# Which engine makes the low halves of the weight splits: thirteen units from DMA to VectorE, one unit in which the heads pause, and two subtractions of w_out one unit later

## The chip, the cores and the metric

The kernel runs on one core of one Trainium2 chip. The metric is the device time in microseconds (us) of one execution; of the kernel before three executions are shown, with a median of 689.74 us (689.03 to 690.15). One more execution was profiled.

## What is computed

One layer of a hybrid encoder on x of 512 tokens by 1024 channels, all in float32:

```
h = rmsnorm(x, norm_w)
proj = h @ w_in + b_in                      # 1024 x 11272
mq, mk, mv, mi, mf, mo, mz, sq, sk, sv, sz, gates = split(proj)
# branch A: matrix memory, 4 heads of 256, causal conv and SiLU on mq, mk
y_m = rmsnorm(mlstm(conv(mq), conv(mk), mv, mi, log_sigmoid(mf))) * sigmoid(mo) * silu(mz)
# branch B: stick-breaking attention, 8 heads of 128
y_s = stick_breaking(rmsnorm(sq), rmsnorm(sk), sv) * silu(sz)
merged = sigmoid(g_m) * (y_m @ w_proj_m) + sigmoid(g_s) * (y_s @ w_proj_s)
out = x + merged @ w_out
```

## The kernel before

**Units.** All large products are cut into units: 128 output channels with the whole depth of 1024, or 512 output channels with 256 of the depth. A unit's weights (512 KB) are loaded into a tile `stg` (three buffers), split there into a high part `wh` and a low part `wl` (three buffers each, rounded to float32r), and multiplied in three passes, high by high, high by low and low by high (`mm3`, L94 to L97). A full unit is 24 matmuls of 128x512, in two halves of 12. The units stand in one list and are worked in its order; the loop at L1498 counts them as c. E is 36 (L29). The places that matter here, by c:

- 40 to 43 (E+4 to E+7) are q of the second set of attention heads, 44 to 47 its k, 48 to 51 its SiLU gate z, 52 to 55 a part of the merge gates;
- 100 to 107 are w_proj_s, 108 to 115 w_proj_m (n_proj is 116), and behind them come the products with w_out, which are formed with sums and differences of its blocks (t1 to t4, L1224 to L1241).

**The two ways to make a low part.** `Unit.split` (L122) has ScalarE write the high part with one ACTIVATE. Then either VectorE subtracts (L101: `wl = st - wh`), or, where `by_dma` is set, ScalarE writes minus the high part into `wl` with a second ACTIVATE (L128), and a DMA that GpSimd issues adds the tile `st` to it (L129, 512 KB, accumulating). That DMA still reads `stg`, so the buffer comes free only when it has landed. L1197 chooses the units of the second kind: before, all eight of w_proj_m and sixteen around the second set's q, k, z and gates, c = 40 to 55.

**What sets the order.** Each engine works its queue in the order of the code. In step c the loop calls what is due in that step (the table `later`), evacuates the banks of unit c-1, calls `ahead(c)`, which splits unit c+2 and issues loads up to unit c+4, issues the first half of unit c's matmuls, then lets every active head do one step (L1528), and issues the second half. From c = 108 on `ahead` also runs ahead of the evacuation (L1506). A head is a generator (L471): its steps are query and key parts; scores; a scan chain over two row blocks on VectorE (L519, L520, L537); the chain over the two others; a store of the weights `ay` to DRAM; their reload as `az`; a step without work; the split of `az` into `ath` and `atl`; the product with v in two steps (`aps<-ath,vh` and so on), the last with L593 on VectorE. The set `REST` (L34) names the steps c in which heads do nothing.

**The k group's end.** Units 44 to 47 fill all four dense PSUM banks (`dps`). In step 48 VectorE reads the four banks (L388, `kraw`), ScalarE squares each (L405, sixteen instructions with their accumulator reads in two steps), GpSimd makes the reciprocal roots (L283, L284), and one step later VectorE scales `kraw` by them (L420). Unit 48 needs the first of those banks. The two halves of `kraw` are thus scaled in steps 49 and 50, and in step 50 TensorE transposes `kraw` for the next head (L482).

Of the kernel before, what the change touches and what calls it, by code (L numbers as in the profile page):

```python
# [28 lines left out]
E = 4 + FILL + 14 * PAIRS  # L29
# [1 line left out]
M_START = [E + n for n in (37, 41, 54, 60)]  # L31
GATES_PREP, GATES_START, GATES_SCAN = E - 3, E - 1, E + 26
TURNED = {("q", 0, 0), ("q", 0, 1), ("q", 1, 0), ("q", 1, 1), ("k", 0, 1), ("k", 1, 1)}
REST = {E + n for n in (48,)}  # L34
AHEAD, LOADS = 2, 4


# [1 line left out]
def tile_hybrid_layer(  # L39
# [93 lines left out]
    units = []  # L133
# [844 lines left out]
    class Pair:  # L978
# [24 lines left out]
        def at(self, c, fn, *a):  # L1003
            later.setdefault(c, []).append(lambda: fn(*a))
# [189 lines left out]

    chan_group(w_proj_m, 0, D, lambda k: ymp[k], pm_evac)
    n_proj = len(units)
    for un in units[n_proj - 8:] + units[E + 4:E + 20]:  # L1197
        un.by_dma = True


# [170 lines left out]
    for g in range(2):  # L1371
        at(-11 + g, w_load, "B22", g, "P5")
        at(-12 + 2 * g, w_load, "B12", g, "A")
        at(-9 + g, w_load, "B11", g, "A")
        at(-8 + 2 * g, t3, g)
        at(-6 + 2 * g, t2, g)
        at(-5 + 2 * g, t1, g)
        at(1 + g, t4, g)
# [119 lines left out]
    for c in range(N):  # L1498
# [29 lines left out]
        for g in list(act):  # L1528
            if c in REST:
                continue  # L1530
            if next(g, "end") == "end":
                act.remove(g)
        for e in list(pend):
            if c >= e[0] and e[2]():
                pend.remove(e)
                g = e[3]()
# [36 lines left out]
```

## Time and profile before

| | us |
|---|---|
| median of three executions | 689.74 |
| the profiled execution | 688.95 |
| its span, first to last instruction | 687.1 |
| TensorE matmuls busy in the span | 674.7 |
| VectorE busy | 483.2 |
| ScalarE busy | 384.4 |
| GpSimd busy | 128.7 |

The granted TensorE clock was 0.997 over the span. A row of the timeline gives start, duration, engine, line, operation, tiles written and read, and in brackets the idle time ahead of it with what ended it. Matmuls follow each other every 0.227 us, and their durations overlap, so a wait is read from the distance between two starts. DVE is VectorE, ACT is ScalarE, POOL is GpSimd, PE is TensorE, SP issues most of the DMAs.

### The profile page before, as it was taken

How to read it: one execution, taken by the hardware profiler on the slowest of the kernel's cores; microseconds unless marked ns; L12 is line 12 of the kernel's file. 1: busy time of each engine (PE TensorE's matmuls, PEld its weight loads, DVE VectorE, ACT ScalarE, POOL GpSimd, SP SyncE). 2: the span in 40 equal slices, each digit the busy share in tenths (PEclk: the TensorE clock that was granted, in tenths of full speed). 3: DMA queues.
4: the chain of work that ended last, by engine and by line, in shares of the span. 5: the costliest groups of instructions: out<-in, count | busy, mean ns of one | idle time of the engine just before them, and what ended most of it. 6: DMA issues, size and time to landing. Idle time of an engine off the chain costs nothing.

```text
span 687.1 us, 9385 instructions
## 1 busy us (share of the span) xinstructions
PE 674.7 (98%) x3114; PEld 560.6 (82%) x3114; DVE 483.2 (70%) x839; ACT 384.4 (56%) x715; POOL 128.7 (19%) x278
## 2 busy tenths in 40 slices
PE   8999999999998899999999999999999999999998
PEld 6888888878887788888888888888888888778876
DVE  6777778668568468878788655479964466355997
ACT  7576545477694675653654747344465854335451
POOL 4023121423382234310011011100000120111020
PEclk9999999999999999999999999999999999999999
DMA  7576793958999999738369532535344478998433
GB/s 251 141 235 161 245 248 90 231 176 188 264 247 249 254 241 254 211 115 207 93 123 199 128 107 62 156 94 145 83 137 148 128 221 260 238 260 209 145 81 103
DMA packets 136336, 122.47 MB, mean 178 GB/s; under 512 B 17578, under 2 KB 106052, under 8 KB 136288
## 3 DMA queue, kind: packets, MB, share of 16 engines
q1 hardware_dynamic: 129232, 101.82, 50.7%
q0 software_dynamic: 6912, 19.93, 15.6%
q8 instruction: 24, 0.39, 0.2%
q14 instruction: 24, 0.20, 0.1%
q10 hardware_dynamic: 144, 0.13, 0.1%
HBM read 83.00 MB, written 18.93 MB: 148 GB/s over the span
## 4 chain that ended last, share of the span: by engine, by line
PE 80%; DMA 9%; issue 3%; DVE 2%; ACT 2%; POOL 1%; SPq 1%; POOLq 0%; ACTq 0%; DVEq 0%
PE dps L97 19%; PE dps L95 19%; PE dps L96 19%; PE dps L971 5%; DMA wl<-stg 4%; PE aps L971 4%; PE aps L96 3%; PE aps L97 3%; PE aps L95 3%; DMA stg<-in_w_proj_m_dram 2%; DMA stg<-in_w_in_dram 2%; ACT sqj L405 1%; PE dps L1446 1%; PE dps L1447 1%; PE dps L1448 1%
## 5 line engine op out<-in xcount | busy, mean ns | idle before, releaser
L95 PE MATMUL dps<-hh,wh 128*128 128x512 f32 x448 | 176.1, 393 | 1.7 <-DVE kraw L388 1.7
L97 PE MATMUL dps<-hh,wl 128*128 128x512 f32 x448 | 175.2, 391 | 2.1 <-DMA wl<-stg 2.1
L96 PE MATMUL dps<-hl,wh 128*128 128x512 f32 x448 | 175.1, 391 | 0.0
L101 DVE TENSOR_TENSOR wl<-stg,wh 128x1024 fp32r<-128x1024 f32 x60 | 73.3, 1222 | 58.0 <-ACT wh L100 57.3
L97 PEld LDWEIGHTS dps<-hh,wl 128*128 128x128 f32 x448 | 84.5, 189 | 20.6 <-DMA wl<-stg 2.6
L95 PEld LDWEIGHTS dps<-hh,wh 128*128 128x128 f32 x448 | 84.4, 188 | 18.7 <-DVE kraw L388 2.1
L96 PEld LDWEIGHTS dps<-hl,wh 128*128 128x128 f32 x448 | 84.5, 189 | 16.8
L100 ACT ACTIVATE wh<-stg 128x1024 fp32r<-128x1024 f32 x60 | 63.0, 1052 | 20.1 <-PE dps L96 12.9
L127 ACT ACTIVATE wh<-stg 128x1024 fp32r<-128x1024 f32 x24 | 25.3, 1054 | 33.7 <-DMA stg<-in_w_proj_m_dram 13.1
L129 POOL DMA_DIRECT2D wl<-stg x24 | 21.2, 882 | 106.8 <-ACT wl L128 74.2
L743 ACT ACTIVATE tmp<-acc 128x512 f32<-128x512 f32 x16 | 10.1, 633 | 52.9 <-DVE acc L740 52.9
L95 PE MATMUL dps<-wh,hh 128*128 128x512 f32 x96 | 37.5, 391 | 0.0
L96 PE MATMUL dps<-wl,hh 128*128 128x512 f32 x96 | 37.4, 390 | 0.0
L97 PE MATMUL dps<-wh,hl 128*128 128x512 f32 x96 | 37.4, 390 | 0.0
L740 DVE SCALAR_TENSOR_TENSOR acc<-tmp,vec,acc 128x511 f32<-128x511 f32 (+2 forms) x48 | 36.0, 750 | 1.7
L97 PE MATMUL dps<-yh,wl 128*128 128x512 f32 x64 | 25.3, 395 | 1.5 <-DMA wl<-stg 1.5
L519 DVE TENSOR_TENSOR_SCAN om<-om 128x512 f32<-128x512 f32 (+3 forms) x32 | 26.3, 822 | 0.0
L128 ACT ACTIVATE wl<-stg 128x1024 fp32r<-128x1024 f32 x24 | 25.1, 1045 | 0.0
L96 PE MATMUL dps<-yl,wh 128*128 128x512 f32 x64 | 24.9, 390 | 0.0
L95 PE MATMUL dps<-yh,wh 128*128 128x512 f32 x64 | 24.9, 389 | 0.0
L101 DVE TENSOR_TENSOR atl<-az,ath 128x384 fp32r<-128x384 f32 (+1 forms) x24 | 13.8, 601 | 14.9 <-ACT ath L100 10.6
L863 ACT ACTIVATE hns<-aps,hst 128x256 f32<-128x256 f32 x16 | 7.6, 475 | 27.8 <-DVE hst L862 20.8
(303 smaller groups left out, 1547.9 us busy)
## 6 DMA issues: line engine op xcount, KB each, us to landing
stg<-in_w_in_dram SPq DMA_DIRECT2D x71, 512.0 KB, 4.9
wl<-stg POOLq DMA_DIRECT2D x24, 512.0 KB, 7.2
a_d<-ay SPq DMA_DIRECT2D x8, 640.0 KB
az<-a_d SPq DMA_DIRECT2D x32, 160.0 KB, 5.4
stg<-in_w_proj_s_dram SPq DMA_DIRECT2D x8, 512.0 KB
B<-in_w_out_dram SPq DMA_DIRECT2D x8, 512.0 KB, 12.9
stg<-in_w_proj_m_dram SPq DMA_DIRECT2D x8, 512.0 KB, 3.9
dst<-u POOLq DMA_DIRECT2D x12, 256.0 KB, 4.7
```

The lines of the kernel that those rows point to most:

```text
L95: nc.tensor.matmul(ps, ah, bh, start=first, stop=False)
L96: nc.tensor.matmul(ps, ah, bl, start=False, stop=False)
L97: nc.tensor.matmul(ps, al, bh, start=False, stop=last)
L100: nc.scalar.activation(hi, src, AF.Copy)
L101: nc.vector.tensor_tensor(lo, src, hi.bitcast(F32), op=OP.subtract)
L127: nc.scalar.activation(self.wh, self.st, AF.Copy)
L128: nc.scalar.activation(self.wl, self.st, AF.Copy, scale=-1.0)
L129: nc.gpsimd.dma_start(out=self.wl, in_=self.st, accum_op=OP.add)
L519: nc.vector.tensor_tensor_scan(back, back, back, 1.0, op0=OP.mult, op1=OP.bypass)
L740: nc.vector.scalar_tensor_tensor(acc[:, j:], t[:, 0:T - j], cw(3 - j, ch), acc[:, j:], op0=OP.mult, op1=OP.add)
L743: nc.scalar.activation(t, acc, AF.Sigmoid)
L971: nc.tensor.matmul(pr.bank[key, tb], a, w[:, i, :], start=begin and n == 0, stop=end and n == 2, skip_group_check=again)
```

## The change

Three lines are edited:

```
-REST = {E + n for n in (48,)}
+REST = {E + n for n in (11, 48)}
...
-    for un in units[n_proj - 8:] + units[E + 4:E + 20]:
+    for un in units[n_proj - 3:] + [units[E + n] for n in (4, 5, 6, 7, 9, 10, 11, 12)]:
         un.by_dma = True
...
-        at(-8 + 2 * g, t3, g)
+        at(-7 + 2 * g, t3, g)
```

Of the 24 units whose low part came by DMA, eleven keep it: 40 to 43, 45 to 48, and 113 to 115. Thirteen go over to VectorE: 44, 49 to 55, and 108 to 112. Each of these loses one ACTIVATE (L128) and one DMA of GpSimd (L129) and gains one subtraction on VectorE (L101). In step 47 the three heads then active do nothing, so each of their later steps comes one unit later. The difference t3 of two blocks of w_out is taken in steps 109 and 111 and no longer in 108 and 110.

VectorE around steps 47 and 48, before. The rows begin with the end of step 46 (`ay` is a head's transposed weights); `atl` to the second `ay` are step 47's head work, then step 48 evacuates the k group:

```order
L537 STREAM_TRANSPOSE ay<-a_all 128x4x32
L101 TENSOR_TENSOR atl<-az,ath 128x384
L519 SCALAR_TENSOR_TENSOR om<-om 128x256
L520 TENSOR_TENSOR a_all<-a_all,om 128x256
L537 STREAM_TRANSPOSE ay<-a_all 128x4x32 x2
L519 SCALAR_TENSOR_TENSOR om<-om 128x384
L520 TENSOR_TENSOR a_all<-a_all,om 128x384
L537 STREAM_TRANSPOSE ay<-a_all 128x4x32 x3
L388 TENSOR_TENSOR kraw<-dps,brow 128x512 x4
L432 STREAM_TRANSPOSE ty<-qraw 128x8x32 x4
```

The same place in the changed kernel:

```order
L537 STREAM_TRANSPOSE ay<-a_all 128x4x32
L101 TENSOR_TENSOR wl<-stg,wh 128x1024
L388 TENSOR_TENSOR kraw<-dps,brow 128x512 x4
L432 STREAM_TRANSPOSE ty<-qraw 128x8x32 x4
L101 TENSOR_TENSOR wl<-stg,wh 128x1024
L101 TENSOR_TENSOR atl<-az,ath 128x384
L519 SCALAR_TENSOR_TENSOR om<-om 128x256
L520 TENSOR_TENSOR a_all<-a_all,om 128x256
L537 STREAM_TRANSPOSE ay<-a_all 128x4x32 x2
L519 SCALAR_TENSOR_TENSOR om<-om 128x384
L520 TENSOR_TENSOR a_all<-a_all,om 128x384
L537 STREAM_TRANSPOSE ay<-a_all 128x4x32 x3
```

The seven rows of head work have moved behind the evacuation of `kraw`, and two low parts (units 49 and 50) stand in the queue, one ahead of the evacuation and one behind it.

VectorE in steps 49 and 50, as the difference of the two orders, from the end of step 48 on:

```order
+L374 SCALAR_TENSOR_TENSOR ys<-dps,bvec,tmp 128x512
+L420 TENSOR_SCALAR kraw<-kraw,rk 128x128 x8
+L101 TENSOR_TENSOR wl<-stg,wh 128x1024
 L593 TENSOR_TENSOR ys<-aps,ys 128x512
-L374 SCALAR_TENSOR_TENSOR ys<-dps,bvec,tmp 128x512
-L420 TENSOR_SCALAR kraw<-kraw,rk 128x128 x8
-L101 TENSOR_TENSOR atl<-az,ath 128x512
-L101 TENSOR_TENSOR atl<-az,ath 128x384
 L374 SCALAR_TENSOR_TENSOR ys<-dps,bvec,tmp 128x512
 L452 TENSOR_SCALAR tz<-tz,qkw 128x1024
 L420 TENSOR_SCALAR kraw<-kraw,rk 128x128 x8
+L101 TENSOR_TENSOR wl<-stg,wh 128x1024
```

The low part of unit 51 now stands ahead of the second scaling of `kraw`, that of unit 52 behind it, and the next head's `atl` (two rows) has gone behind both.

## The prediction

> **What bounds the kernel now.** I read the page first, then who waited for whom on TensorE, then TensorE's timeline around each wait.
>
> ```profile
> PE 674.7 (98%) x3114; PEld 560.6 (82%) x3114; DVE 483.2 (70%) x839; ACT 384.4 (56%) x715; POOL 128.7 (19%) x278
> ...
> PE dps L97 <- DMA wl<-stg: 3.6, 3, 2.1
> PE dps L95 <- DVE kraw L388: 1.7, 1, 1.7
> ```
>
> TensorE is busy for 98% of the span, and the change leaves every matmul in place. So it can gain only waits, and two kinds stand at its places: for low parts by DMA, three times, and for VectorE's read of a `kraw` bank, once.
>
> ```profile
> 214.87 0.39 PE L96 MATMUL dps<-wl,hh 128*128 128x512 f32 x1
> 215.09 0.39 PE L97 MATMUL dps<-wh,hl 128*128 128x512 f32 x1
> 217.21 0.50 PE L95 MATMUL dps<-hh,wh 128*128 128x512 f32 x1 [1.72 <-DVE kraw L388]
> ...
> 229.19 0.39 PE L96 MATMUL dps<-hl,wh 128*128 128x512 f32 x1
> 231.73 0.50 PE L97 MATMUL dps<-hh,wl 128*128 128x512 f32 x1 [2.15 <-DMA wl<-stg]
> ...
> 232.81 0.63 PE L97 MATMUL dps<-hh,wl 128*128 128x512 f32 x1
> ...
> 235.37 0.50 PE L97 MATMUL dps<-hh,wl 128*128 128x512 f32 x1
> 235.71 0.39 PE L95 MATMUL aps<-ath,vh 128*128 128x512 f32 x1
> ...
> 236.94 0.60 PE L482 MATMUL aps<-ident,kraw 128*128 128x128 f32 x4
> ...
> 599.24 0.39 PE L96 MATMUL dps<-yl,wh 128*128 128x512 f32 x1
> 600.47 0.50 PE L97 MATMUL dps<-yh,wl 128*128 128x512 f32 x1 [0.84 <-DMA wl<-stg]
> ...
> 616.70 0.39 PE L96 MATMUL dps<-yl,wh 128*128 128x512 f32 x1
> 617.73 0.50 PE L97 MATMUL dps<-yh,wl 128*128 128x512 f32 x1 [0.65 <-DMA wl<-stg]
> ```
>
> Starts normally lie 0.23 apart, so the four waits cost their distance less 0.23: 1.89 at unit 48's first matmul, 2.31 in unit 50, 1.00 in unit 108 and 0.80 in unit 111. After the longest the matmuls run slow: from 231.73 to 235.37 there are nine steps of matmuls, 3.64 us where nine at 0.227 take 2.04. That is another 1.60. The stretches show why (columns: PE, PEld, DVE, ACT, POOL, then the granted clock, the DMA share, GB/s):
>
> ```profile
> 208.00:218.00 10.00, 8.28 (x37) 6.60 (x36) 9.45 (x23) 3.15 (x7) 0.87 (x1) 1.00 1.02 259
> 232.00:236.00 4.00, 4.00 (x12) 3.13 (x12) 3.17 (x11) 1.83 (x3) 0.86 (x1) 0.57 1.04 234
> 590.00:606.00 16.00, 15.16 (x67) 12.26 (x66) 5.32 (x8) 5.22 (x7) 2.64 (x3) 1.00 1.01 233
> ```
>
> The clock fell to 0.57 behind the 2.15 us gap and stayed at 1.00 around the 1.72 us gap, so here it falls somewhere between the two. [...] The waits and the clock sum to 1.89 + 2.31 + 1.60 + 1.00 + 0.80 = 7.60 us. The DMA engines are full at both places.
>
> **The change: low parts of units 49 to 55 and 44 by VectorE.** One low part costs VectorE 1.22 us and spares ScalarE 1.05 us, a GpSimd issue and a transfer:
>
> ```profile
> L101 DVE TENSOR_TENSOR wl<-stg,wh 128x1024 fp32r<-128x1024 f32 x60 | 73.3, 1222 | 58.0 <-ACT wh L100 57.3
> L127 ACT ACTIVATE wh<-stg 128x1024 fp32r<-128x1024 f32 x24 | 25.3, 1054 | 33.7 <-DMA stg<-in_w_proj_m_dram 13.1
> L128 ACT ACTIVATE wl<-stg 128x1024 fp32r<-128x1024 f32 x24 | 25.1, 1045 | 0.0
> ...
> 222.75 8.94 DMA wl<-stg
> ...
> 590.46 9.96 DMA wl<-stg
> ...
> 608.87 8.81 DMA wl<-stg
> ```
>
> The first group row's own idle time says what VectorE's subtraction waits for, ScalarE's high part. The split is issued two units ahead, at least 10.9 us, so 1.22 us in place of 8.94 removes the 2.31 wait in unit 50, and the slow clock behind it. Unit 44's subtraction falls ahead of the chain of step 42, beside matmuls that need nothing of it soon; I cost it at nothing.
>
> **The pause in step 47.** VectorE's queue of that place before (rows as above: start, duration):
>
> ```profile
> 212.15 0.52 DVE L101 TENSOR_TENSOR atl<-az,ath 128x384 fp32r<-128x384 f32 x1
> ...
> 215.88 0.70 DVE L537 STREAM_TRANSPOSE ay<-a_all 128x128 f32<-128x128 f32 x3
> 216.50 2.44 DVE L388 TENSOR_TENSOR kraw<-dps,brow 128x512 f32<-128x512 f32 x4
> 218.87 1.40 DVE L432 STREAM_TRANSPOSE ty<-qraw 128x256 f32<-128x256 f32 x4
> 220.91 0.69 DVE L593 TENSOR_TENSOR ys<-aps,ys 128x512 f32<-128x512 f32 x1 [0.64 <-PE aps L97]
> ...
> 231.13 0.74 DVE L374 SCALAR_TENSOR_TENSOR ys<-dps,bvec,tmp 128x512 f32<-128x512 f32 x1
> 231.79 0.74 DVE L452 TENSOR_SCALAR tz<-tz,qkw 128x1024 f32<-128x1024 f32 x1
> 232.45 1.66 DVE L420 TENSOR_SCALAR kraw<-kraw,rk 128x128 f32<-128x128 f32 x8
> 234.02 0.55 DVE L101 TENSOR_TENSOR atl<-az,ath 128x384 fp32r<-128x384 f32 x1
> 234.49 0.69 DVE L101 TENSOR_TENSOR qtt<-tz,qtt 128x512 fp32r<-128x512 f32 x1
> ```
>
> Head work of 216.50 − 212.15 = 4.35 us stands ahead of `kraw`. Now only the low part of unit 49 does: 212.15 + 1.2 = 213.3, and the first bank is read by 213.95. On TensorE unit 47 loses six matmuls of its heads (235.71 to 236.94 are six such: 1.23), so its last one starts at 215.09 − 1.23 = 213.86 and unit 48 could start at 214.09. The 1.89 wait goes but for a tenth. The moved matmuls come back in unit 48, at no gain or loss.
>
> **What is late next.** ScalarE stands between `kraw` and the rest:
>
> ```profile
> 224.31 0.30 ACT L405 ACTIVATE sqj<-kraw 128x128 bf16<-128x128 f32 x1
> ...
> 227.42 0.19 ACT L405 ACTIVATION_READ_ACCUMULATOR sqj<-kraw 128x1 f32 x1
> ```
>
> The squares of two banks take 3.30 us (224.31 to 227.61). From 213.95 they end at 217.3, unit 50's high part at 218.3, its low part on VectorE at 219.5 (which stands idle for it from 217.0), the moved head work of 4.35 at 223.9. Then come L374 (0.7), the first scaling (1.6), unit 51's low part (1.2), L593 (0.6), L374 and L452 (0.66 each, their starts' distance) and the second scaling (1.6): 230.9. TensorE meanwhile: unit 48 takes 24 × 0.227 + 1.23 = 6.7 and ends at 220.8; unit 49 takes 5.45 and six smaller matmuls of 256 and 128 columns, about 1.23 × 384/896 = 0.53, and ends at 226.8; twelve matmuls later, at 229.5, it reaches the transposes of `kraw` (L482). They wait 230.9 − 229.5 = 1.4 us. The trace of before has this wait hidden: the second scaling ended at 234.02, and TensorE, without 2.31 + 1.60 of its own waits, would have come at 236.94 − 3.91 = 233.03. It can be nothing (if ScalarE's pieces close up by 1.4) or twice that, 2.8, if two more pieces of 0.7 slip in; I take 1.4.
>
> Steps 51 to 55 each get 1.22 us more on VectorE, and the last two steps of two heads come one unit later, where the next heads' scan chains stand. Step 52 then holds L374, L452, a low part, L593, two `atl` (1.1), a chain of 3.9 (the 4.35 above less its `atl`) and two splits (`qtt` and its like, 0.69 each): about 9.6 us in a unit of 7. The excess of 2.6 meets the 2.7 us by which the twelve matmuls of the next unit's first half run ahead of its scores. Bounds are 0 and 1.5 (one low part more than fits); I take 0.5, nearer to none because the excess just fits.
>
> [...] In the trace GpSimd's masks stretch beside VectorE's scan:
>
> ```profile
> 246.81 0.29 POOL L512 TENSOR_SCALAR_AFFINE_SELECT a_all<-a_all 128x128 f32<-128x128 f32 x1
> ...
> 251.45 1.43 POOL L509 TENSOR_SCALAR_AFFINE_SELECT om<-om 128x128 f32<-128x128 f32 x1
> ...
> 251.47 1.34 DVE L519 TENSOR_TENSOR_SCAN om<-om 128x512 f32<-128x512 f32 x1
> ```
>
> A mask of 0.29 can take 1.43, 1.14 more. If a new subtraction did that to a mask on the path of steps 51 to 55, it would be inside the 1.5. [...]
>
> **w_proj_m.** VectorE is busy 5.32 of 16 us there (row above), so 1.22 per unit has room, and low parts of units 108 and 111 are ready long ahead of use: 1.00 and 0.80 go. It also frees `stg` some 8 us earlier, where the load queue stood:
>
> ```profile
> SPq L120 <- DMA wl<-stg: 26.4, 5, 10.3
> ```
>
> SP waited 26.4 us in 585 to 625 for low parts to land. Units 113 to 115 keep the DMA; nine to ten us from issue fit into two units (10.9) less ScalarE's 2.1 only just, so between 0 and 0.8 may return; 0, since the full queue loses five transfers. t3 moves by a unit and is needed by t2 one step later; its 1.22 us lie in the same idle time.
>
> **Sum.** 7.60 − 0.1 − 1.4 − 0.5 = 5.6 us. Against the profiled execution, 688.95 us, that is 683.35. The median of before is 0.79 higher, so 684.1 us.
>
> **The rivals.**
> - No new wait: the chain through ScalarE and VectorE closes up. 689.74 − 7.6 = 682.1. For it speaks the load taken off ScalarE and the DMA engines; against it the 233.03 above. 0.18.
> - The wait at the transposes passes the length at which the clock falls. It takes another 1.0 us in the chain, say a reload or GpSimd's roots held up: 2.4 of wait and 1.6 of slow clock in place of 1.4, so 686.7. [...] 0.12.
> - The waits in w_proj_m are not for the low parts' route but for the full DMA engines, and the loads come late instead: 1.8 is not won, 685.9. Against it: SP's 26.4 us of waiting is for low parts. 0.06.
> - Slower: VectorE's queue stands. The subtraction waits for ScalarE, which waits for a load; if those of units 50 to 53 landed 3 us late each, the heads behind them would stand 12 us, less the 2.7 that TensorE has in hand, plus one fall of the clock: 10.9 lost against 7.6 won, 693.0. It decides from some 2.5 us a unit on. For it: the full DMA engines; against it: eight transfers fewer there. 0.05.
>
> **The numbers.** The forecast's own chance is 0.59. Its range: new waits from 0.3 to 3.5 us put it between 682.4 and 685.6. With the rivals but the slower one, and the executions of before lying 1.1 apart, the range is 681.5 to 687.0. A measurement of this kernel can tell about 0.2%, 1.4 us, from no change. Slower has 0.05 from the last rival, the same 0.05 from the tails of the others, faster 0.9.
>
> **What would show it.** Right: no TensorE wait for `wl<-stg`, none over 0.4 at unit 48, no stretch of low clock, and a new wait of about 1.4 at L482 near 230, named after VectorE's L420. Wrong: a low clock after that wait, TensorE waiting for `wl` from VectorE, or waits at scores (`ktt`) near 250 to 265 that sum to more than 1.5. A time over 688.4 would refute the sum as a whole.

## The result

The kernel after takes 681.7 us (median of 9 executions, 680.71 to 686.68) against 689.66 us of before (9 executions, 687.34 to 694.84): ratio 0.9898, 95% interval 0.9864 to 0.9932. The medians lie 8.0 us apart; the ratio stands for 7.0 us less (4.7 to 9.4). The forecast was 684.1, so the direction was right and the gain, by the medians, 2.4 us too small. Six more executions, made beside the last experiments below, gave 681.19 against 688.65: ratio 0.9902 (0.9869 to 0.9934).

The execution of after that was profiled took 686.68 us, one of two among the nine that lie some 5 us above the others. Its profile lost them near 145 us, ahead of everything that the change moves (where the other, 686.65, lost them is not on record); so one of the six later executions of the same kernel (680.82 us, span 679.1) stands beside it and is called the second profile.

From the page of after, first profile: the engines, the subtractions and the low-part DMAs.

```profile
PE 673.8 (98%) x3114; PEld 561.4 (82%) x3114; DVE 497.3 (73%) x852; ACT 372.5 (54%) x702; POOL 114.9 (17%) x265
L101 DVE TENSOR_TENSOR wl<-stg,wh 128x1024 fp32r<-128x1024 f32 x73 | 89.2, 1222 | 69.5 <-ACT wh L100 68.8
L129 POOL DMA_DIRECT2D wl<-stg x11 | 9.8, 888 | 89.6 <-DVE gback L1177 45.9
```

Thirteen subtractions of 1.22 us more (x60 to x73) and thirteen DMAs fewer (x24 to x11): the change did what it says. What TensorE still waits for behind the first 20 us, by the waits of PE in the second profile (total, times, longest, in us):

```profile
PE aps L482 <- DVE dst L420: 0.5, 1, 0.5
PE aps L96 <- DVE ktt L101: 0.4, 1, 0.4
PE aps L482 <- DVE kraw L420: 0.2, 1, 0.2
```

Neither `wl<-stg` nor `kraw L388` is left, and the one new wait, the last row, is 0.2. TensorE at the two places of the forecast, second profile:

```profile
213.92 0.39 PE L97 MATMUL dps<-wh,hl 128*128 128x512 f32 x1
214.14 0.39 PE L95 MATMUL dps<-hh,wh 128*128 128x512 f32 x1
...
229.49 0.40 PE L97 MATMUL dps<-hh,wl 128*128 128x512 f32 x1
229.72 0.49 PE L482 MATMUL aps<-ident,kraw 128*128 128x128 f32 x3
230.37 0.33 PE L482 MATMUL aps<-ident,kraw 128*128 128x128 f32 x1 [0.15 <-DVE kraw L420]
230.45 0.49 PE L95 MATMUL dps<-hh,wh 128*128 128x512 f32 x1
```

And VectorE there:

```profile
212.02 1.20 DVE L101 TENSOR_TENSOR wl<-stg,wh 128x1024 fp32r<-128x1024 f32 x1
213.13 2.48 DVE L388 TENSOR_TENSOR kraw<-dps,brow 128x512 f32<-128x512 f32 x4
...
227.92 0.75 DVE L374 SCALAR_TENSOR_TENSOR ys<-dps,bvec,tmp 128x512 f32<-128x512 f32 x1 [0.18 <-ACT tmp L372]
228.59 0.74 DVE L452 TENSOR_SCALAR tz<-tz,qkw 128x1024 f32<-128x1024 f32 x1
229.25 1.65 DVE L420 TENSOR_SCALAR kraw<-kraw,rk 128x128 f32<-128x128 f32 x8
```

Side by side, in us from the start of the span (each the first matmul of a unit by TensorE's timeline):

| | before | forecast | after, second profile |
|---|---|---|---|
| unit 47 | 208.64 | | 208.70 |
| unit 48 | 217.21 | 214.1 | 214.14 |
| unit 49 | 223.53 | 220.8 | 220.82 |
| unit 50 | 228.97 | 226.8 | 227.00 |
| second scaling of `kraw` ends | 234.11 | 230.9 | 230.90 |
| unit 57 | 281.77 | | 276.17 |
| unit 108 | 599.01 | | 593.40 |
| unit 115 | 639.45 | | 631.48 |

By unit 57 the gain is 5.60, nothing changes from there to 108, and in w_proj_m another 2.37 comes: 7.97 in all, of 8.0 between the spans (687.1 and 679.1).

**The 5 us near 145.** In the first profile TensorE waits for the scaled keys of the first set of heads, by its timeline:

```profile
145.12 0.39 PE L97 MATMUL dps<-hh,wl 128*128 128x512 f32 x1
147.94 0.47 PE L482 MATMUL aps<-ident,dst 128*128 128x128 f32 x1 [2.43 <-DVE dst L420]
```

The two stretches behind it, by the windows (start and end; then length, busy time of PE, of its weight loads PEld, of DVE, ACT and POOL; then the clock, third number from the end), run at half speed:

```profile
147.76:151.18 3.42, 2.93 (x9) 2.25 (x10) 3.42 (x11) 0.79 (x2) 0.00 (x0) 0.50 0.50 153
151.18:154.59 3.41, 3.41 (x10) 2.64 (x9) 0.41 (x1) 0.00 (x0) 0.00 (x0) 0.50 0.51 154
```

Ahead of it the chain of waits has the load of a unit's weights (start, duration), first in the first profile, then in the second:

```profile
131.41 9.08 DMA stg<-in_w_in_dram
```

```profile
130.07 7.41 DMA stg<-in_w_in_dram
```

It was issued 1.34 later and took 1.67 longer; ScalarE's squares stand in its queue behind the split of that unit, so the scaling came 3.0 later. Before has the same wait with 0.5 us in its profile. Why the load is later in some executions stays open.

### The profile page after: what moved, and what is told of

The parts are those of the page before. It is cut to its first block, busy times and chain, and to the rows that moved or that the text cites. A ratio compares the mean times of both kernels' runs of the same rounds, so it can differ in the third digit from the quotient of the medians.

```text
span 685.0 us, 9337 instructions
## 1 busy us (share of the span) xinstructions
PE 673.8 (98%) x3114; PEld 561.4 (82%) x3114; DVE 497.3 (73%) x852; ACT 372.5 (54%) x702; POOL 114.9 (17%) x265
## 4 chain that ended last, share of the span: by engine, by line
PE 91%; DMA 2%; DVE 2%; ACT 2%; issue 1%; POOL 1%; SPq 1%; DVEq 0%; ACTq 0%; POOLq 0%
PE dps L95 23%; PE dps L97 22%; PE dps L96 22%; PE dps L971 5%; PE aps L971 4%; PE aps L96 3%; PE aps L97 3%; PE aps L95 3%; DMA stg<-in_w_in_dram 2%; PE dps L1446 1%; PE dps L1448 1%; PE dps L1447 1%; ACT sqj L405 1%; PE aps L853 1%; PE aps L855 1%
## 5 line engine op out<-in xcount | busy, mean ns | idle before, releaser
L101 DVE TENSOR_TENSOR wl<-stg,wh 128x1024 fp32r<-128x1024 f32 x73 | 89.2, 1222 | 69.5 <-ACT wh L100 68.8
L100 ACT ACTIVATE wh<-stg 128x1024 fp32r<-128x1024 f32 x73 | 76.7, 1052 | 42.9 <-PE dps L96 22.5
L129 POOL DMA_DIRECT2D wl<-stg x11 | 9.8, 888 | 89.6 <-DVE gback L1177 45.9
L507 ACT ACTIVATE om<-aps,rq 128x512 f32<-128x512 f32 (+3 forms) x32 | 16.7, 523 | 14.3 <-PE aps L97 14.3
L509 POOL TENSOR_SCALAR_AFFINE_SELECT om<-om 128x128 f32<-128x128 f32 x32 | 14.5, 452 | 44.5 <-ACT om L507 44.3
L101 DVE TENSOR_TENSOR atl<-az,ath 128x384 fp32r<-128x384 f32 (+1 forms) x24 | 13.8, 603 | 10.4 <-ACT ath L100 6.1
```

The lines of the kernel that those rows point to most:

```text
L100: nc.scalar.activation(hi, src, AF.Copy)
L101: nc.vector.tensor_tensor(lo, src, hi.bitcast(F32), op=OP.subtract)
L129: nc.gpsimd.dma_start(out=self.wl, in_=self.st, accum_op=OP.add)
L507: nc.scalar.activation(om[:, 0:n], zp, AF.Sigmoid, scale=rn[:, h:h + 1])
L509: nc.gpsimd.affine_select(out=om[:, ts], in_=om[:, ts], compare_op=OP.is_gt, fill=1.0, base=0, channel_multiplier=1, pattern=[[-1, 128]])
```

## The experiments

"Ratio" is to the kernel before in the same group of executions, with its 95% interval. Three groups of four ran on three chips, with medians of before of 687.91 (29 executions), 688.73 (11) and 688.65 (11).

### The parts alone

**The pause alone.**

```
-REST = {E + n for n in (48,)}
+REST = {E + n for n in (11, 48)}
```

> The kernel before with the pause in step 47 alone; all 24 low parts stay with the DMA. Theory A (the transfer of unit 50's low part starts when ScalarE has squared the first kraw banks, so it starts as much earlier as kraw is read): the wait at unit 48's first matmul goes (-1.9 us), the one in unit 50 shrinks from 2.3 to about 1.6, and the clock no longer falls (-1.6): some 4 us faster, ratio near 0.994. Rival B (the full DMA engines set the landing, not the issue): TensorE only comes earlier to the same landing, waits some 4 us in unit 50, the clock falls as before, and the time stays within 1 us: ratio 0.999 to 1.001. In both the waits of 1.0 and 0.8 us in w_proj_m stay.

Measured: 689.01 us, ratio 1.0016 (0.9991 to 1.0042). Both theories fell. The waits at units 48 and 50 were gone in the profile, yet nothing was won, since a new wait stood at the scores of the next heads, and the clock fell behind it:

```profile
253.45 0.39 PE L95 MATMUL aps<-ktt,qtt 128*128 128x512 f32 x1
256.39 0.50 PE L96 MATMUL aps<-ktt,qtt 128*128 128x512 f32 x1 [2.55 <-DVE ktt L101]
```

```profile
254.21:257.62 3.41, 1.23 (x8) 1.15 (x9) 3.17 (x8) 2.08 (x4) 0.99 (x2) 1.00 0.83 238
257.62:261.03 3.41, 3.41 (x10) 2.69 (x9) 3.03 (x8) 1.32 (x4) 2.08 (x6) 0.50 0.98 221
```

`ktt` stands in VectorE's queue behind `atl` and a scan chain, `atl` behind ScalarE's `ath`, and that waited for turned data to come back from DRAM:

```profile
249.22 1.05 ACT L100 ACTIVATE ath<-az 128x512 fp32r<-128x512 f32 x2 [3.42 <-DMA az<-a_d]
```

**The subtractions of units 44 and 49 to 55 alone, without the pause.**

```
-    for un in units[n_proj - 8:] + units[E + 4:E + 20]:
+    for un in units[n_proj - 8:] + [units[E + n] for n in (4, 5, 6, 7, 9, 10, 11, 12)]:
```

> The kernel before with the low parts of units 44 and 49 to 55 by VectorE, without the pause; w_proj_m as before. Theory A (the pause is needed, since the new subtraction of unit 49 stands ahead of the read of kraw): no wait in unit 50, but the wait at unit 48's first matmul grows by 1.2 us to about 3 us, and the clock falls behind it (1.6 us, one stretch of 3.4 us at half speed): -2.3 - 1.6 + 1.2 + 1.6, some 1 us faster, ratio 0.998. [...]

Measured: 687.01 us, ratio 0.9992 (0.9969 to 1.0015). The profiled execution is the slowest of the twelve (693.04: it also lost time near 145 and waited 3.7 us in w_proj_m), so its rows show the mechanism and not the size. In it unit 48's first matmul waits a microsecond longer than before, as theory A has it, and the stretch behind it, from 222.79 to 226.20, runs at half speed:

```profile
218.82 0.39 PE L97 MATMUL dps<-wh,hl 128*128 128x512 f32 x1
221.89 0.50 PE L95 MATMUL dps<-hh,wh 128*128 128x512 f32 x1 [2.68 <-DVE kraw L388]
```

```profile
219.38:222.79 3.41, 0.90 (x4) 0.77 (x5) 3.27 (x8) 0.81 (x4) 0.00 (x0) 1.00 1.10 249
222.79:226.20 3.41, 3.41 (x10) 2.63 (x9) 2.16 (x6) 3.25 (x13) 2.03 (x4) 0.50 1.04 236
618.74:622.15 3.41, 1.49 (x7) 0.91 (x5) 3.17 (x5) 1.08 (x2) 0.00 (x0) 1.00 1.05 209
```

By the first two rows the clock fell from 1.00 to 0.50 behind the gap of 2.68. (The last row, another place of the same run, is taken up at the end.)

**Both together.** The two edits above.

> The kernel before with the pause and with the low parts of units 44 and 49 to 55 by VectorE; w_proj_m as before. Theory A: both waits near 217 and 231 and the half-speed stretch go, the transposes of kraw wait about 0.4 us: -5.6 us, ratio 0.992. It is the sum of the parts only if pause and subtractions don't hang together; if they do (rival of the two runs above: each part alone worth little), this run gains more than the sum of the two runs with one part each. The waits of 1.0 and 0.8 us in w_proj_m stay.

Measured: 684.68 us, ratio 0.9951 (0.9934 to 0.9968), 3.4 us faster (2.2 to 4.5). Neither part alone can be told from no change (1.0016 and 0.9992, both intervals with 1 in them); together they gain clearly. The size is short of the 5.6: three of the six executions lie at 683.5 to 683.8, the other three at 685.5 to 685.9 with clocks of 0.997 and 0.998, and the profiled one of these (0.998) has the wait near 145 (2.4). On the other side, the half speed at 232 that I counted in full isn't in every execution of before: 16 of the 29 here have a clock of 0.999 or more, and one such stretch alone makes 0.9975 (half of 3.41 us in 687).

**w_proj_m and t3 alone.**

```
+    for un in units[n_proj - 3:] + units[E + 4:E + 20]:
...
+        at(-7 + 2 * g, t3, g)
```

> The kernel before with the low parts of the first five units of proj_m by VectorE and the two subtractions for w_out one step later; all else as before. Theory A (these waits are for the route of the low parts): the waits of 1.0 and 0.8 us in units 108 and 111 go, 1.8 us faster, ratio 0.9974. Rival (the full DMA engines delay the loads instead): the same TensorE waits stand there, now for VectorE's wl, and the time is within 0.5 us of before.

Measured: 686.97 us, ratio 0.9981 (0.9964 to 0.9998), 1.3 us faster. TensorE is never idle there (first column of busy time, us of 16):

```profile
592.00:608.00 16.00, 16.00 (x72) 13.27 (x71) 8.75 (x11) 4.34 (x6) 0.00 (x0) 1.00 0.90 259
608.00:624.00 16.00, 16.00 (x72) 13.23 (x71) 12.77 (x18) 7.38 (x9) 1.78 (x2) 1.00 0.44 106
```

Theory A stands, the rival falls: the waits were for the low parts' route. (The two parts of the change, 3.4 and 1.3, sum to 4.7, the lower edge of the 4.7 to 9.4 for the whole; whether they add up exactly the times can't tell.)

### What the pause alone ran into

**The transfers taken away, ScalarE's second pass kept.** The kernel after with, for units 44 and 49 to 55:

```
+            elif self.by_act:
+                nc.scalar.activation(self.wh, self.st, AF.Copy)
+                nc.scalar.activation(self.wl, self.st, AF.Copy, scale=-1.0)
+                nc.vector.tensor_tensor(self.wl, self.st, self.wh.bitcast(F32), op=OP.subtract)
```

> The kernel after, in which ScalarE still writes a negative copy of the high part for units 44 and 49 to 55, as it did for the DMA's sum, though VectorE then overwrites it: the transfers are gone, ScalarE's 1.05 us per unit are kept. Theory A (what hurt the pause alone was the transfers: full DMA engines held up the second heads' turned data, and ScalarE and VectorE stood in their queues for it): as the kernel after, ratio to before 0.989 to 0.992, and no wait over 1 us at the scores near 253. Rival (ScalarE's second pass was it): a wait of 2 to 3 us at the scores near 253 and ratio 0.995 or more. Between them: the pass delays VectorE's subtraction by 1.05 us each, so waits of up to 1 us at the transposes of kraw may come.

Measured: 683.77 us, ratio 0.9935 (0.9911 to 0.9959). The time lies above the range of theory A, though four of the six executions are at 682.3 to 684.1; in the profiled one TensorE also waits 2.4 us in the kernel's first 11 us, where after has 1.1 to 1.2. The profile is plainer behind that: no TensorE wait over 0.7 us at any scores, and the same `ath` now starts without waiting for its data:

```profile
247.35 1.03 ACT L100 ACTIVATE ath<-az 128x512 fp32r<-128x512 f32 x2
```

So the wait of the pause alone came of the low parts' transfers, not of ScalarE's 1.05 us per unit. With them the data came back too late for heads that had been put off by a unit: in the pause alone SyncE waited 3.7 us for the store of these weights (`a_d<-ay`) to land and issued the loads of `az` from 240.37 on; here it issued them from 233.74 on.

**Unit 50 by DMA again.** The kernel after with 14 added to the list of units by DMA.

> The kernel after with the low part of unit 50 by DMA again, the one for which TensorE waited 2.3 us in the profile of before; the other twelve stay with VectorE. Theory A (the wait came of full DMA engines, with six transfers close together, not of the route): alone in a quieter place the transfer takes 6 to 7 us for 8.9, lands before TensorE needs it, and the time is that of the kernel after within 0.5 us; no wait for a low part in unit 50, and the wait at the transposes gets shorter, as VectorE has 1.2 us less ahead of it. Rival (the route itself is too slow for two units ahead): a wait of 1 to 2 us in unit 50, in part of the runs with a fall of the clock, 1 to 4 us slower than after.

Measured: 681.47 us, ratio 0.9905 (0.9872 to 0.9938), beside 681.19 of after. TensorE doesn't wait for it. GpSimd's issue of that part, and from the view of the DMAs for 218 to 250 its time to landing:

```profile
219.91 0.93 POOL L129 DMA_DIRECT2D wl<-stg  x1 [0.81 <-ACT wl L128]
```

```profile
wl<-stg POOLq DMA_DIRECT2D x1, 512.0 KB, 7.1
```

It is issued 2.84 earlier than before (222.75), since `kraw` is read earlier, and takes 7.1 for 8.94; it lands at 227.0, a microsecond ahead of its first use. So theory A holds in part only: of the 4.7 us, 2.84 are the earlier start. Its other expectation missed: the wait at the transposes stayed at 0.2, though VectorE had 1.2 us less to do.

### Prices and limits

**2.44 us more on VectorE ahead of the second scaling.** The kernel after with

```
+                for _ in range(self.more):
+                    nc.vector.tensor_tensor(self.wl, self.st, self.wh.bitcast(F32), op=OP.subtract)
...
+    units[E + 15].more = 2
```

> The kernel after, in which VectorE makes the low part of unit 51 three times over (the same result): 2.44 us more in its queue ahead of the second scaling of kraw. [...] Rival B (a gap longer than some 2 us always costs the clock, as the prediction had it): +4 us in every run, no run at 1.000. [...] Rival D (VectorE has slack there): the wait stays under 1 us.

Measured: 684.49 us, ratio 0.9947 (0.9928 to 0.9965). The transposes (here L485), and the windows around them:

```profile
231.13 0.38 PE L485 MATMUL aps<-ident,kraw 128*128 128x128 f32 x2
233.20 0.33 PE L485 MATMUL aps<-ident,kraw 128*128 128x128 f32 x1 [1.70 <-DVE kraw L423]
233.99 0.33 PE L485 MATMUL aps<-ident,kraw 128*128 128x128 f32 x1 [0.46 <-DVE kraw L423]
234.07 0.48 PE L95 MATMUL dps<-hh,wh 128*128 128x512 f32 x1
```

```profile
231.69:235.10 3.41, 1.44 (x7) 1.08 (x8) 3.41 (x11) 1.23 (x2) 0.00 (x0) 1.00 0.96 268
235.10:238.51 3.41, 3.41 (x10) 2.67 (x9) 2.83 (x5) 0.00 (x0) 0.00 (x0) 0.50 1.12 250
```

From the first transpose to the next matmul it is 2.94, of which the four transposes of before take 0.35 (236.94 to 237.29): 2.59 of waiting. Without the extra work it is 0.73, or 0.38. So 2.21 of the 2.44 reach TensorE, and rival D falls. The clock fell in this profile (0.50 from 235.10 to 238.51), and three of the six executions show 1.000 (683.83, 684.06, 684.77), so rival B's loss in every run falls too.

**No low part by DMA.** The kernel after with `un.by_dma = False`.

> The kernel after with all low parts by VectorE, none by DMA (units 40 to 43, 45 to 48 and 113 to 115 too). Theory A (VectorE is full in steps 44 to 47, so each low part more there delays the first read of kraw, which has no slack left in the kernel after): unit 48 waits 1.2 to 2.4 us for kraw, and other waits of up to 1 us come at scores between 195 and 215; 2 to 4 us slower than the kernel after, ratio to before 0.993 to 0.996. Rival (VectorE has room for these too): no wait at unit 48, ratio 0.989 to 0.990.

Measured: 682.92 us, ratio 0.9929 (0.9902 to 0.9955). Unit 48 starts 1.09 behind the matmul ahead of it, a wait of 0.86:

```profile
215.03 0.39 PE L97 MATMUL dps<-wh,hl 128*128 128x512 f32 x1
216.12 0.47 PE L95 MATMUL dps<-hh,wh 128*128 128x512 f32 x1 [0.70 <-DVE kraw L388]
```

Between theory and rival: the place is right, the price is below the 1.2 to 2.4 that I gave. VectorE can carry nearly all low parts; by the wait at unit 48 the eleven left to the DMA are worth about a microsecond, which the intervals can't confirm.

**t3 back in steps 108 and 110.** The kernel after with `at(-8 + 2 * g, t3, g)`.

> The kernel after with the two subtractions for w_out back in steps 108 and 110. Theory A (VectorE is idle for 1 to 2 us a unit there, and the low parts stand ahead of these subtractions in each step): no TensorE wait in w_proj_m, same time as the kernel after within 0.3 us. Rival (the subtraction of 1.22 us holds up the low part of the unit after): a wait of up to 1.2 us for VectorE's wl in units 109 to 112.

Measured: 682.13 us, ratio 0.9909 (0.9878 to 0.9939). No wait for a low part, but one that I had not named, for the low part of the first half of `ym`, which stands behind t3's 1.22 us:

```profile
598.26 0.39 PE L95 MATMUL dps<-ymh,wh 128*128 128x512 f32 x1
598.86 0.50 PE L96 MATMUL dps<-yml,wh 128*128 128x512 f32 x1 [0.21 <-DVE yml L101]
```

That is 0.37; the medians differ by 0.9 from after, within both intervals. The move of t3 is worth 0.4 by the profile, and the times can't tell it from nothing.

### A faster version

**The first head one step later.** The kernel after with

```
-SB_START = [E + n for n in (1, 3, 6, 8, 14, 16, 18, 20)]
+SB_START = [E + n for n in (2, 3, 6, 8, 14, 16, 18, 20)]
```

> The kernel after with the first head one step later (38 for 37), to take away the wait at the transposes near 145, which stands in both kernels (0.8 us in the profile of before, 3.3 us and a stretch of 6.8 us at half speed in that of after, where a weight load landed 3 us later). Theory A (the head has that much slack, since it waits for its v in later steps anyway): no wait near 145, 1 us faster than the undisturbed runs of after, no run 5 us above the others, ratio to before 0.986 to 0.988. Rival (the scan chain of the first head then falls into one step with the second's, and the wait only moves to the scores near 150 to 160): ratio 0.989 to 0.993 and waits for ktt there.

Measured: 680.55 us (four executions, 680.32 to 681.24), ratio 0.9883 (0.9866 to 0.9901). In the third group it ran again, beside the kernel after:

> The kernel after once more, unchanged, beside the next three on one chip. Every theory expects a ratio to before of 0.988 to 0.992; runs at a clock of 1.000 near 681.5 us, and one run in four or five some 5 us above them with a clock of 0.994 to 0.995, from the wait near 145.

> The kernel with the first head one step later, once more, now beside the kernel after on one chip. Theory A (the wait near 145 is gone for good): 1 us faster than the undisturbed runs of after, ratio to before near 0.9885, and no run 5 us above the others. Rival (the four runs without one were luck): a run in four or five some 5 us above the others here too.

Measured: after 681.19 us (680.82 to 684.47), the version 679.93 us (679.59 to 681.18), ratio 0.988 (0.9847 to 0.9912). The first transposes run through, in the version's timeline:

```profile
149.89 0.60 PE L482 MATMUL aps<-ident,dst 128*128 128x128 f32 x4
150.24 0.48 PE L95 MATMUL dps<-hh,wh 128*128 128x512 f32 x1
...
211.31 0.39 PE L97 MATMUL dps<-wh,hl 128*128 128x512 f32 x1
212.11 0.47 PE L95 MATMUL dps<-hh,wh 128*128 128x512 f32 x1 [0.40 <-DVE kraw L388]
```

It is 1.26 us faster than after in the medians, and five of its six executions here lie below the fastest of after's six; none of its ten lies 5 us up, of after's fifteen two do and one 3 us. Part is given back at unit 48, which now waits 0.57. It beats both kernels.

## Why the prediction was right, and where it was not

**Right: what goes.** The time lies in the stated range of 681.5 to 687.0, near its lower end, and below the 682.4 to 685.6 that the forecast's own new waits left. In the profiles all five terms of the 7.60 are gone: the waits at units 48 and 50, the half-speed stretch, the two in w_proj_m. That the stretch's 1.60 could be counted in full is luck in part, since 16 of the 29 executions of before in the first group don't show it. The starts of units 48 and 49 and the end of the second scaling came within 0.1 us of the walk through the queues, unit 50 within 0.2.

**The step that failed: "They wait 230.9 − 229.5 = 1.4 us."** The scaling did end at 230.90. But the transposes don't wait for its end. Each reads one head's columns of one bank, and the scaling is eight pieces, four to a bank, 0.2 us apart: the last transpose needs the first piece of the second bank, the fifth of the eight, at 229.25 + 5 × 0.2 = 230.3. It ran at 230.37; the other three started at 229.72 with no wait. So the term is 0.38, not 1.4. That it did not shrink when VectorE had less to do (unit 50 by DMA) has a reason in the rows above: L374 ahead of the scaling waited 0.18 for ScalarE's `tmp`, which follows unit 49's last matmul. From unit 49's end (L372 starts at 227.20) to the fifth piece it is 3.1 us through L372, L374, L452 and the pieces, and TensorE's half unit takes 12 × 0.227 = 2.7, whatever stands ahead on VectorE.

**Mis-sized: steps 51 to 55 and w_proj_m.** The gain by unit 57 was 5.60. The removed 5.80 less 0.38 is 5.42, so nothing is left of the 0.5 for steps 51 to 55; the 2.6 us of excess met 2.7 us of room, and the room held. In w_proj_m 2.37 came where 1.80 was counted: I priced only the two longest gaps of units 108 and 111, while whole units were 1.13 (6.57 to 5.44), 0.95 (6.39 to 5.44) and, unit 113, 0.28 longer than without. In before the matmul behind such a wait also comes a tenth late (600.47 to 600.80, 0.33 for 0.23), which my distances left out, and unit 113 had a wait of its own (0.14 at 628.89). The terms: 1.0 for the transposes, 0.5 for the later steps, 0.6 for w_proj_m and the 0.1 kept at unit 48 make 2.2 of the 2.4 that lie between 5.6 and 7.97; the rest is tenths that I can't assign.

**The rivals.** "No new wait", which had 0.18, came nearest, 682.1 against 681.7: the new waits are 0.4 in all where the forecast had 2.0. "The wait at the transposes grows" did not come, but the run with two more subtractions shows its price: 2.21 us for 2.44 of work, and in its profile 3.41 us at a clock of 0.50. "w_proj_m's waits are for the loads" is refuted by the run of that part alone. "VectorE's queue stands" did not come; the run with all low parts on VectorE shows 0.86 us as the first sign of it.

**What I had not seen.** I costed the pause and the subtractions as terms that add up. They don't: without the subtractions the pause lost its gain again at the scores near 253, since late data met heads that were a unit later; without the pause the subtraction of unit 49 stood ahead of `kraw`.

**The masks.** GpSimd's masks did not stretch. Their rows, before and then after (first profile):

```profile
L509 POOL TENSOR_SCALAR_AFFINE_SELECT om<-om 128x128 f32<-128x128 f32 x32 | 16.9, 527 | 23.3 <-ACT om L507 23.1
```

```profile
L509 POOL TENSOR_SCALAR_AFFINE_SELECT om<-om 128x128 f32<-128x128 f32 x32 | 14.5, 452 | 44.5 <-ACT om L507 44.3
```

Thirteen more subtractions, and a mask takes 452 ns in the mean for 527. Neither the subtractions nor the fewer DMA issues are needed for that, since the pause alone, with all 24 issues and no subtraction added, has it too:

```profile
L509 POOL TENSOR_SCALAR_AFFINE_SELECT om<-om 128x128 f32<-128x128 f32 x32 | 14.2, 445 | 27.9 <-ACT om L507 27.7
```

So three profiles with the pause have 445, 452 and, the second of after, 454, and before, without it, has 527. Here it goes with the pause; what the masks fell beside, before and after, was not followed up.

## What to carry to other kernels

When two edits each remove a wait, walk the queues for the two together and for each alone: the worth of a pause can lie in another edit that makes the later place fit. When an operation waits for the product of a loop, count which piece of the loop it needs; a wait for the fifth of eight pieces was 0.38 us where the forecast had taken the whole loop and 1.4. And when TensorE is busy for 98% of the span, look in several executions for a wait that is long in only some of them: one here cost some 5 us in the execution that was profiled, and one number in a list of start steps removed it.

## What the runs showed of the hardware

The prediction put the fall of the clock "somewhere between" a gap of 1.72 us and one of 2.15. The gaps of the runs don't sort that way. Before, at the two long waits of the profile that the forecast used (second number: TensorE's busy time of 3.41; third from the end: clock):

```profile
215.11:218.52 3.41, 1.69 (x8) 1.10 (x7) 3.27 (x9) 1.21 (x6) 0.00 (x0) 1.00 1.05 234
...
228.77:232.18 3.41, 1.26 (x6) 0.76 (x5) 2.13 (x4) 3.41 (x6) 1.19 (x2) 1.00 1.09 263
232.18:235.59 3.41, 3.41 (x10) 2.66 (x9) 2.99 (x11) 1.66 (x3) 0.86 (x1) 0.50 1.02 227
```

Behind the gap of 2.15 the clock was 0.50 from 232.18 to 235.59, for 3.41 us; behind the gap of 1.72 it stayed at 1.00 (218.52 to 225.34). In the profile of before these 3.41 us are the only stretch at half speed ahead of the last microsecond; in the first profile of after it is the 6.83 us from 147.76 to 154.59, at the gap of 2.43, ahead of the last two. The rows above show three more: 3.41 us at 0.50 behind a gap of 2.55 (the pause alone, from 257.62), behind one of 2.68 (the subtractions alone, from 222.79) and behind two of 1.70 and 0.46 (two more subtractions, from 235.10).

At two other gaps no such stretch followed. In the run of the subtractions alone the row from 618.74 to 622.15 holds most of a gap of 2.00, at a clock of 1.00, and behind it, to 625.56, the clock is 1.00 too. In the run with ScalarE's second pass kept there is a gap of 2.39 in the first 11 us:

```profile
10.51 0.47 PE L1453 MATMUL dps<-fh,hh 128*128 128x512 f32 x1 [2.39 <-DVE hh L323]
```

That profile has a clock of 0.999 over its span of 682.3 us, where 3.41 us at half speed alone make 0.9975. So here a gap of 2.39 passed without a fall, and two gaps of 1.70 and 0.46 had one behind them. What decides it was not shown. The executions of one kernel differ as well: of the six with the two more subtractions three have a clock of 1.000, the others 0.998 (the profiled one), 0.997 and 0.995; which gaps cost the last two their clock is not on record.
